# A decoder trunk on one core: the fourth gate and up group moved ahead of the first down groups, every middle block turned by DMA

## The chip, the cores and the metric

The kernel runs on one core of one Trainium2 chip. The metric is device time in microseconds for one execution of the whole program, the median over runs; smaller is better. Engine names are the profile's: PE is TensorE's matmul, PEld its weight load, DVE is VectorE, ACT is ScalarE, POOL is GpSimd, SP is SyncE, whose queue issues almost all DMAs here. "L420" is line 420 of the kernel before.

## The reference

Two pre-norm residual layers over 256 positions of width 2048, in float32. Each layer has a mixer (layer 0: sliding-window attention beside an mLSTM; layer 1: forgetting attention) and a SwiGLU feed-forward block (FFN) with 5632 hidden columns. Only the FFN is touched:

```python
D_MODEL = 2048
SEQ = 256
DEPTH = 2
FFN_HIDDEN = -(-(8 * D_MODEL) // (3 * 256)) * 256      # 5632

def swiglu(xn, w_gate, w_up, w_down):
    return (jax.nn.silu(xn @ w_gate) * (xn @ w_up)) @ w_down

def reference(...):
    h = x
    for layer in range(DEPTH):
        ...
        h = h + mix.astype(h.dtype)
        h = h + swiglu(rms_norm(h, norm_ffn[layer]), w_gate[layer], w_up[layer], w_down[layer])
    return rms_norm(h, norm_final)
```

## The kernel before

**Precision.** Every float32 operand is split into a high and a low half (`hi`, `lo` for weights; `xh`, `xl` for the normed input; `mh`, `ml` for the hidden block), and a product takes three matmuls of 128 rows by 512 columns (`three`, L417 to L420). ACT casts the high half (L167, L293), DVE subtracts for the low half (L168, L294). So each weight chunk of 512 KB (two k tiles by 512 columns) costs an ACT and a DVE instruction before PE can use it.

**Groups.** `pair_group` multiplies 256 rows by two blocks of 512 columns at once. It walks over pairs of k tiles in a given order of positions; a position is either plain (24 matmuls) or mixed (a Strassen-like form with 21 matmuls, more ACT and DVE work, and sums of the left operand, `sx` or `sd`, that must be ready). In the plain positions the results gather in four PSUM banks, `plain`; the mixed ones also fill four banks `prods` of the other half of PSUM. The argument `par` says which half; consecutive groups alternate. At the end the `prods` are evicted into the tile `c` (L549 on ACT, L550 to L553 on DVE). The tile `c` has one buffer.

**The FFN.** The hidden width is eleven blocks of 512 columns. A gate and up group (eight positions, five plain and three mixed, 183 matmuls) makes one block: after it `plain` is added to `c` (L578), SiLU is taken (L580) and gate times up is formed (L582). The block then has to be turned, since the down product contracts over it. `PARTS = (0, 3, 7, 11)` cuts the eleven blocks into three parts. Each part runs its gate and up groups, then two down groups (columns 0 to 1023 and 1024 to 2047 of the output) that contract over the blocks of the part and add into the residual `h` (L675, L299). Part one has three blocks, twelve k tiles, and so down groups of six positions (four plain, two mixed, 138 matmuls); parts two and three have four blocks, and down groups of eight positions.

**Two ways to turn a block.** The usual way is by DMA: ACT copies the 16-bit halves of `c` apart into `flat` (L605, twice), SP issues two DMA transposes (`turn_planes`, L246), and later a closure `join` puts the halves together on ACT (L251, twice), splits them into `mh` and `ml` (L293, L294) and forms the sums `sd` (`sums_of`, L235 to L238). `join` is issued at position `MID` (6) of the next gate and up group, or at `MID_DOWN` (5) of the part's first down group. The last block of part one alone (`g == g1 - 1 and nk < 16`, L585) goes another way: PE transposes it against the identity in eight instructions (L591) into two banks `pf`, and ACT and DVE split from there.

**Order.** The program is written in the order just told; the framework's scheduler sets the order of the instructions on each engine ahead of time, by a simulated time line, so that matmuls of neighbouring groups are interleaved where operands are not ready. On the chip each engine runs its own list in that fixed order. Weight loads and DMA transposes share SP's queue.

Of the kernel before, what the change touches and what calls it, by code (L numbers as in the profile page):

```python
# [17 lines left out]
P = 128  # L18
# [5 lines left out]
NB = 512  # L24
# [23 lines left out]
TURN_AT = (1, 2, 3, 5)  # L48
TURN_DOWN = (2, 3, 4, 6)
MID = 6  # L50
MID_DOWN = 5
RAWS = 4
PARTS = (0, 3, 7, 11)


def mixed_of(order):
    return [p for w, p in order if w]
# [5 lines left out]
def trunk(  # L63
# [96 lines left out]
    def load_chunk(w, k0, c0, n):  # L160
        raw = ahead.pop(0) if ahead else load_raw(w, k0, c0, n)
        return split_chunk(raw, n)
# [129 lines left out]
    def split_plain(dst_h, dst_l, src):  # L292
        nc.scalar.copy(dst_h, src)  # L293
        nc.vector.tensor_tensor(out=dst_l, in0=src, in1=dst_h.bitcast(F32), op=ALU.subtract)  # L294
# [127 lines left out]
    def bank(par, name):  # L422
        return pm.tile([P, NB], F32, tag="pm", name=name) if par else pa.tile([P, NB], F32, tag="acc", name=name)
# [66 lines left out]
            )  # L490
        sums_of(room, sh, sl, None, full)

    def pair_group(room, par, lhs, sums, mats, order, todo=()):
        plain = [[bank(par, "acc") for _ in range(NT)] for _ in range(2)]
        todo = list(todo)
        prods = None
        kinds = [kind for kind, _ in order]
        t0, t1 = slice(0, P), slice(P, 2 * P)
        for pos, (kind, pair) in enumerate(order):
            k0 = 2 * pair  # L500
            if not kind:
                last = pos == len(order) - 1
                walk = [(i, t) for i in range(CK) for t in range(NT)]
                if last:
                    walk.sort(key=lambda it: it[1])
                for m, (w, c0) in enumerate(mats):
                    hi, lo = load_chunk(w, k0, c0, NB)
                    run_due(todo, pos)
                    for i, t in walk:
                        ah, al = lhs(k0 + i)  # L510
                        ts = slice(t * P, (t + 1) * P)
                        three(
                            plain[m][t], ah[:, ts], al[:, ts], hi[:, i, :], lo[:, i, :],
                            pos == 0 and i == 0, last and i == CK - 1,
                        )
                continue
            first, last = 1 not in kinds[:pos], 1 not in kinds[pos + 1 :]
            if first:
                prods = [bank(1 - par, "prod") for _ in range(4)]
            ra, rb = (room.raw(m, w, k0, c0) for m, (w, c0) in enumerate(mats))  # L520
            hg, lg = split_chunk(ra, NB)
            run_due(todo, pos)
            t4 = room.t4()
            nc.vector.tensor_tensor(out=t4[:, 0, :], in0=rb[:, 0, :], in1=ra[:, 0, :], op=ALU.subtract)
            nc.vector.tensor_tensor(out=t4[:, 1, :], in0=rb[:, 1, :], in1=rb[:, 0, :], op=ALU.subtract)
            hu = wp.tile([P, CK, NB], F32R, tag="hi", name="hi")
            lu = wp.tile([P, CK, NB], F32R, tag="lo", name="lo")
            split_plain(hu[:, 1, :], lu[:, 1, :], rb[:, 1, :])
            nc.vector.tensor_tensor(out=rb[:, 0, :], in0=rb[:, 1, :], in1=t4[:, 0, :], op=ALU.subtract)
            nc.vector.tensor_tensor(out=rb[:, 1, :], in0=ra[:, 1, :], in1=rb[:, 0, :], op=ALU.subtract)  # L530
            ht, lt = [], []
            for two in (t4, rb):
                hs, ls = room.two()
                split_plain(hs, ls, two)
                ht += [hs[:, 0, :], hs[:, 1, :]]
                lt += [ls[:, 0, :], ls[:, 1, :]]
            sh, sl = sums(pair)
            xa, la = lhs(k0)
            xb, lb = lhs(k0 + 1)
            three(prods[0], xa[:, t0], la[:, t0], hg[:, 0, :], lg[:, 0, :], first, last)  # L540
            three(plain[0][0], xb[:, t0], lb[:, t0], hg[:, 1, :], lg[:, 1, :], False, False)
            three(plain[1][0], sh[:, 3, :], sl[:, 3, :], hu[:, 1, :], lu[:, 1, :], False, False)
            three(prods[1], sh[:, 0, :], sl[:, 0, :], ht[0], lt[0], first, last)
            three(prods[2], sh[:, 2, :], sl[:, 2, :], ht[1], lt[1], first, last)
            three(prods[3], sh[:, 1, :], sl[:, 1, :], ht[2], lt[2], first, last)
            three(plain[0][1], xb[:, t1], lb[:, t1], ht[3], lt[3], False, False)
        c = room.c()
        u2 = room.tmp([P, NB], "u2")
        nc.scalar.copy(c[:, 0, :], prods[0])  # L549
        nc.vector.tensor_tensor(out=u2, in0=prods[3], in1=c[:, 0, :], op=ALU.add)  # L550
        nc.vector.tensor_tensor(out=c[:, 1, :], in0=prods[2], in1=u2, op=ALU.add)  # L551
        nc.vector.tensor_tensor(out=c[:, 2, :], in0=prods[1], in1=u2, op=ALU.add)
        nc.vector.tensor_tensor(out=c[:, 3, :], in0=prods[1], in1=c[:, 1, :], op=ALU.add)  # L553
        return plain, c

    def ffn(layer, fp, room, pending, sx, sd, key, idx_next=None, key_next=None, finish=None, then=None):
# [3 lines left out]
            j = mixed_of(ORDER).index(pair)  # L560
            return sx[0][:, j, :, :], sx[1][:, j, :, :]

        for g0, g1 in zip(PARTS, PARTS[1:]):
            end = g1 == PARTS[-1]
            nk = 4 * (g1 - g0)
            order = DOWN[nk // 2]
            todo = list(zip(TURN_AT, pending))
            pending = []
            for g in range(g0, g1):
                par = (g1 - 1 - g) % 2  # L570
                plain, c = pair_group(
                    room, par, x_of, sums_x, [(w_gate[layer], g * NB), (w_up[layer], g * NB)], ORDER, todo
                )
                todo = []
                for m in range(2):
                    for t in range(NT):
                        o = c[:, 2 * m + t, :]
# [3 lines left out]
                for t in range(NT):  # L581
                    nc.vector.scalar_tensor_tensor(  # L582
                        out=c[:, t, :], in0=c[:, 2 + t, :], scalar=r[:, t : t + 1], in1=c[:, t, :], op0=ALU.mult, op1=ALU.mult
                    )
                if g == g1 - 1 and nk < 16:  # L585
                    for half in range(2):
                        pt = bank(par, "pf").rearrange("p (i q) -> p i q", i=2)
                        for i in range(2):
                            cs = (2 * half + i) * P
                            for t in range(NT):  # L590
                                nc.tensor.transpose(pt[:, i, t * P : (t + 1) * P], c[:, t, cs : cs + P], ident)  # L591
                        pair = 2 * (g - g0) + half
                        k = 2 * pair
                        split_plain(mh[:, k : k + 2, :], ml[:, k : k + 2, :], pt)
                        if pair in mixed_of(order):
                            j = mixed_of(order).index(pair)
                            sums_of(
                                room, sd[0][:, j, :, :], sd[1][:, j, :, :], lambda full, pt=pt: nc.scalar.copy(full, pt)
                            )
                    continue  # L600
                cu = c.bitcast(U16).rearrange("p a (n b) -> p a n b", b=2)
                flat = c[:, 2:4, :].bitcast(U16).rearrange("p a n -> p (a n)").rearrange("p (b n) -> p b n", b=2)
                turned = [fp.tile([P, 8, P], U16, tag="tmp", name="turned") for _ in range(2)]
# [1 line left out]
                    nc.scalar.copy(flat[:, b, :].rearrange("p (t n) -> p t n", t=NT), cu[:, 0:2, :, b])  # L605
                turn_planes(turned, flat)

                def join(c=c, turned=turned, g=g, g0=g0, order=order):
                    ct = c[:, 0:2, :].rearrange("p a n -> p (a n)")
                    cb = ct.bitcast(U16).rearrange("p (n b) -> p n b", b=2)  # L610
                    join_planes(cb, turned)
                    k = 4 * (g - g0)
                    split_plain(
                        mh[:, k : k + 4, :].rearrange("p k s -> p (k s)"), ml[:, k : k + 4, :].rearrange("p k s -> p (k s)"), ct
                    )
                    for half in range(2):
                        pair = 2 * (g - g0) + half
                        if pair in mixed_of(order):
                            j = mixed_of(order).index(pair)
                            sums_of(  # L620
                                room,
                                sd[0][:, j, :, :],
                                sd[1][:, j, :, :],
                                None,
                                ct[:, half * 512 : (half + 1) * 512].rearrange("p (i t q) -> p i t q", i=2, t=NT),
                            )

                todo = [(MID if g < g1 - 1 else MID_DOWN, join)]

            def sums_d(pair, order=order):  # L630
                j = mixed_of(order).index(pair)
                return sd[0][:, j, :, :], sd[1][:, j, :, :]

            def close(acc, n):
# [12 lines left out]
            for n0 in (0, 2):  # L647
                if end and idx_next is None and n0 == 2:
# [4 lines left out]
                    continue  # L653
                plain, c = pair_group(
                    room,
                    1 - n0 // 2,
                    m_of,
                    sums_d,
                    [(wd, n0 * NB), (wd, (n0 + 1) * NB)],
                    DOWN_END if end and n0 == 2 else order,  # L660
                    todo + list(zip(TURN_DOWN, pending[0::2] + pending[1::2])),
                )
                todo = []
                pending = []
                if end and idx_next is None:
# [641 lines left out]
```

## Time and profile before

| | |
|---|---|
| median of three runs | 2095.85 us (2094.71 to 2096.68) |
| the profiled execution, its own time | 2093.9 us |
| its span in the profile | 2092.2 us |
| PE busy | 2078.2 us, 99% of the span |
| DVE busy | 1809.4 us, 86% |
| ACT busy | 1358.4 us, 65% |
| DMA transposes issued for the tile `c` | 52 |

The busy time of PE is that of overlapping, pipelined instructions, so it hides what matters here: the distance between the starts of neighbouring matmuls. A row of the time line reads: start, duration, engine, line, operation, tiles, how many instructions are merged in the row, and in brackets how long the engine sat idle before it and which instruction released it. A row of the table by windows reads: the window, its length, and for each engine the busy time and the number of instructions, then the granted TensorE clock and the DMA engines' share.

### The profile page before, as it was taken

What the parts mean: (1) busy time and instruction counts of PE and PEld (TensorE: products, weight loads), DVE (VectorE), ACT (ScalarE), POOL (GpSimd) and SP (SyncE); (2) the same over time, 40 slices, a digit from 0 to 9 for tenths busy, and PEclk for the clock granted to TensorE, in tenths of its full rate; (3) what the DMA queues carried; (4) which work ended last, traced back from release to release, by engine and by line L of the source; (5) the groups of instructions that cost most, each with busy time, mean ns of one, the idle gap of its engine ahead of it and who ended that gap; (6) DMA issues with size and microseconds to landing.
All of it is one profiled execution on the core that took longest, in us unless ns stands there. A gap on an engine that the chain in (4) does not pass through costs nothing.

```text
span 2092.2 us, 26777 instructions
## 1 busy us (share of the span) xinstructions
PE 2078.2 (99%) x9518; PEld 1725.2 (82%) x9518; DVE 1809.4 (86%) x2402; ACT 1358.4 (65%) x1717; POOL 42.0 (2%) x70
## 2 busy tenths in 40 slices
PE   9999999999999999999999999999999999999998
PEld 8878888888888888888888888888888888888886
DVE  6689758998999999998899777679989999999995
ACT  7565568665577656666867676587655667556763
POOL 2100000000000000000000000000000000000000
PEclk9999999999999999999999999999999999999999
DMA  9446667766576657676787775677757676657663
GB/s 332 122 133 211 206 194 225 246 195 197 187 232 220 218 193 226 207 222 173 203 258 200 207 212 170 191 233 229 231 168 228 199 222 211 221 191 229 214 204 128
DMA packets 300214, 433.51 MB, mean 207 GB/s; under 512 B 97825, under 2 KB 106033, under 8 KB 300081
## 3 DMA queue, kind: packets, MB, share of 16 engines
q1 hardware_dynamic: 298320, 426.00, 66.0%
q0 software_dynamic: 1616, 5.78, 0.9%
q8 instruction: 74, 1.21, 0.2%
q14 instruction: 60, 0.48, 0.1%
q10 hardware_dynamic: 144, 0.03, 0.0%
HBM read 408.67 MB, written 2.11 MB: 196 GB/s over the span
## 4 chain that ended last, share of the span: by engine, by line
PE 94%; DVE 3%; issue 1%; DMA 1%; ACT 1%; POOLq 0%; POOL 0%; SPq 0%; ACTq 0%; DVEq 0%
PE acc L418 20%; PE acc L419 20%; PE acc L420 20%; PE prod L418 5%; PE prod L420 5%; PE prod L419 5%; PE acc L195 5%; PE acc L197 5%; PE acc L196 5%; PE vacc L195 1%; PE vacc L196 1%; PE vacc L197 1%; DVE lo L168 1%; PE p L324 0%; DMA raw<-in_w_in_even_dram 0%
## 5 line engine op out<-in xcount | busy, mean ns | idle before, releaser
L167 ACT CAST hi<-raw 128x1024 fp32r<-128x1024 f32 (+1 forms) x664 | 675.1, 1031 | 437.8 <-PE acc L420 223.7
L168 DVE TENSOR_TENSOR lo<-raw,hi 128x1024 fp32r<-128x1024 f32 (+1 forms) x664 | 784.2, 1196 | 137.7 <-ACT hi L167 136.2
L419 PE MATMUL acc<-lo,xh 128*128 128x512 f32 x1204 | 468.7, 389 | 0.5 <-DVE lo L168 0.5
L420 PE MATMUL acc<-hi,xl 128*128 128x512 f32 x1204 | 465.7, 389 | 0.0
L418 PE MATMUL acc<-hi,xh 128*128 128x512 f32 x1204 | 463.2, 390 | 0.8 <-DVE c L551 0.8
L418 PEld LDWEIGHTS acc<-hi,xh 128*128 128x128 f32 x1204 | 225.9, 188 | 49.2 <-DVE c L551 1.6
L419 PEld LDWEIGHTS acc<-lo,xh 128*128 128x128 f32 x1204 | 226.0, 188 | 47.9 <-DVE lo L168 0.8
L420 PEld LDWEIGHTS acc<-hi,xl 128*128 128x128 f32 x1204 | 226.0, 188 | 47.2 <-issue 0.3
L419 PE MATMUL acc<-lo,mh 128*128 128x512 f32 x444 | 172.8, 389 | 0.0
L420 PE MATMUL acc<-hi,ml 128*128 128x512 f32 x444 | 171.3, 389 | 0.0
L418 PE MATMUL acc<-hi,mh 128*128 128x512 f32 x444 | 169.6, 389 | 0.0
L293 ACT CAST ht<-t 128x1024 fp32r<-128x1024 f32 x94 | 98.9, 1052 | 52.7 <-PE prod L420 44.6
L293 ACT CAST ht<-raw 128x1024 fp32r<-128x1024 f32 x94 | 98.7, 1050 | 45.0 <-PE acc L420 17.9
L195 PE MATMUL acc<-hi,mh 128*128 128x512 f32 x320 | 125.9, 396 | 0.7 <-ACT mh L293 0.7
L196 PE MATMUL acc<-lo,mh 128*128 128x512 f32 x320 | 124.9, 390 | 0.0
L197 PE MATMUL acc<-hi,ml 128*128 128x512 f32 x320 | 124.5, 392 | 0.0
L294 DVE TENSOR_TENSOR lt<-raw,ht 128x1024 fp32r<-128x1024 f32 x94 | 114.4, 1217 | 10.8 <-ACT ht L293 10.8
L294 DVE TENSOR_TENSOR lt<-t,ht 128x1024 fp32r<-128x1024 f32 x94 | 114.3, 1216 | 5.0 <-ACT ht L293 4.9
L293 ACT CAST hi<-raw 128x512 fp32r<-128x512 f32 x112 | 69.3, 619 | 73.5 <-PE acc L420 53.9
L419 PEld LDWEIGHTS acc<-lo,mh 128*128 128x128 f32 x444 | 83.3, 188 | 17.3
L418 PEld LDWEIGHTS acc<-hi,mh 128*128 128x128 f32 x444 | 83.3, 188 | 17.3
L420 PEld LDWEIGHTS acc<-hi,ml 128*128 128x128 f32 x444 | 83.3, 188 | 17.2
(380 smaller groups left out, 3558.6 us busy)
## 6 DMA issues: line engine op xcount, KB each, us to landing
raw<-in_w_gate_dram SPq DMA_DIRECT2D x176, 512.0 KB, 4.7
raw<-in_w_up_dram SPq DMA_DIRECT2D x176, 512.0 KB, 4.8
raw<-in_w_down_dram SPq DMA_DIRECT2D x176, 512.0 KB, 4.9
raw<-in_w_in_odd_dram SPq DMA_DIRECT2D x88, 512.0 KB, 4.8
raw<-in_w_in_even_dram SPq DMA_DIRECT2D x64, 512.0 KB, 4.8
raw<-in_w_out_even_dram SPq DMA_DIRECT2D x32, 512.0 KB, 4.2
raw<-in_w_out_odd_dram SPq DMA_DIRECT2D x32, 512.0 KB, 4.7
raw<-in_w_in_odd_dram SPq DMA_DIRECT2D x8, 272.0 KB, 3.5
```

Source lines behind the costliest of these rows:

```text
L167: latest[0] = nc.scalar.copy(hi[:, :, 0:n], raw[:, :, 0:n])
L168: nc.vector.tensor_tensor(out=lo[:, :, 0:n], in0=raw[:, :, 0:n], in1=hi[:, :, 0:n].bitcast(F32), op=ALU.subtract)
L195: nc.tensor.matmul(o, ah[:, ts], hi, start=(k == 0), stop=False)
L196: nc.tensor.matmul(o, ah[:, ts], lo, start=False, stop=False)
L197: last_mm[0] = nc.tensor.matmul(o, al[:, ts], hi, start=False, stop=(k == k_all - 1))
L293: nc.scalar.copy(dst_h, src)
L294: nc.vector.tensor_tensor(out=dst_l, in0=src, in1=dst_h.bitcast(F32), op=ALU.subtract)
L418: nc.tensor.matmul(o, ah, hi, start=start, stop=False)
L419: nc.tensor.matmul(o, ah, lo, start=False, stop=False)
L420: nc.tensor.matmul(o, al, hi, start=False, stop=stop)
```

## The change

The order of the groups in a layer becomes gate and up 0, 1, 2, 3; the down groups of part one; gate and up 4, 5, 6; the down groups of part two; gate and up 7 to 10; the down groups of part three. Group 3 belongs to part two still: only its place moves. The branch with the PE transposes is gone; the blocks 2 and 3 are turned by DMA as the others. The block that is finished last before a pair of down groups is joined in the first of them, at position 4 in part one and at position 5 in the others.

Since block 3 is turned while the down groups of part one still read k slots 0 to 11 of `mh` and `ml`, it goes to slots 12 to 15, and blocks 4, 5 and 6 to slots 0 to 11: the k slots of part two are rotated by four, the down weights are read at row `(k + 4) % 16`, and the order of positions in part two (`DOWN_TURNED`) leaves block 6 for last. `par` simply alternates. The number of matmuls in the groups, of weight loads and of sums is the same.

```diff
-MID_DOWN = 5
+MID_DOWN = (4, 5, 5)
 RAWS = 4
 PARTS = (0, 3, 7, 11)
+PASS = ((0, 1, 2, 3), (4, 5, 6), (7, 8, 9, 10))
+DOWN_TURNED = ((0, 0), (0, 1), (1, 2), (0, 3), (1, 6), (0, 7), (1, 4), (0, 5))
...
-    def pair_group(room, par, lhs, sums, mats, order, todo=()):
+    def pair_group(room, par, lhs, sums, mats, order, todo=(), row=lambda k: k):
...
-                    hi, lo = load_chunk(w, k0, c0, NB)
+                    hi, lo = load_chunk(w, row(k0), c0, NB)
...
-        for g0, g1 in zip(PARTS, PARTS[1:]):
+        par, todo = 0, list(zip(TURN_AT, pending))
+        pending = []
+        for part, (g0, g1) in enumerate(zip(PARTS, PARTS[1:])):
             end = g1 == PARTS[-1]
             nk = 4 * (g1 - g0)
-            order = DOWN[nk // 2]
-            todo = list(zip(TURN_AT, pending))
-            pending = []
-            for g in range(g0, g1):
-                par = (g1 - 1 - g) % 2
+            order = (DOWN[6], DOWN_TURNED, DOWN[8])[part]
+            for g in PASS[part]:
                 plain, c = pair_group(
                     room, par, x_of, sums_x, [(w_gate[layer], g * NB), (w_up[layer], g * NB)], ORDER, todo
                 )
-                todo = []
+                par = 1 - par
...
-                if g == g1 - 1 and nk < 16:
-                    for half in range(2):
-                        pt = bank(par, "pf").rearrange("p (i q) -> p i q", i=2)
-                        for i in range(2):
-                            cs = (2 * half + i) * P
-                            for t in range(NT):
-                                nc.tensor.transpose(pt[:, i, t * P : (t + 1) * P], c[:, t, cs : cs + P], ident)
-                        pair = 2 * (g - g0) + half
-                        k = 2 * pair
-                        split_plain(mh[:, k : k + 2, :], ml[:, k : k + 2, :], pt)
-                        if pair in mixed_of(order):
-                            j = mixed_of(order).index(pair)
-                            sums_of(
-                                room, sd[0][:, j, :, :], sd[1][:, j, :, :], lambda full, pt=pt: nc.scalar.copy(full, pt)
-                            )
-                    continue
...
+                first = PARTS[1] if PARTS[1] <= g < PARTS[2] else (PARTS[2] if g >= PARTS[2] else 0)
+                slot = (g - first + 3) % 4 if first == PARTS[1] else g - first
...
-                    k = 4 * (g - g0)
+                    k = 4 * slot
...
+                    if slot:
+                        sums_of(
+                            room,
+                            sd[0][:, slot - 1, :, :],
+                            sd[1][:, slot - 1, :, :],
+                            None,
+                            ct[:, 0:512].rearrange("p (i t q) -> p i t q", i=2, t=NT),
+                        )
 
-                todo = [(MID if g < g1 - 1 else MID_DOWN, join)]
+                todo = [(MID if g < PASS[part][-1] else MID_DOWN[part], join)]
...
-                    1 - n0 // 2,
+                    par,
                     m_of,
                     sums_d,
                     [(wd, n0 * NB), (wd, (n0 + 1) * NB)],
                     DOWN_END if end and n0 == 2 else order,
                     todo + list(zip(TURN_DOWN, pending[0::2] + pending[1::2])),
+                    row=lambda k, nk=nk, by=4 * (part == 1): (k + by) % nk,
                 )
+                par = 1 - par
```

More of the change, by code (lines that the diff above doesn't have):

```diff
@@ L519, in pair_group @@
                 prods = [bank(1 - par, "prod") for _ in range(4)]
-            ra, rb = (room.raw(m, w, k0, c0) for m, (w, c0) in enumerate(mats))
+            ra, rb = (room.raw(m, w, row(k0), c0) for m, (w, c0) in enumerate(mats))
             hg, lg = split_chunk(ra, NB)
@@ L606, in ffn, with join @@
                 turn_planes(turned, flat)
-                def join(c=c, turned=turned, g=g, g0=g0, order=order):
+                first = PARTS[1] if PARTS[1] <= g < PARTS[2] else (PARTS[2] if g >= PARTS[2] else 0)
+                slot = (g - first + 3) % 4 if first == PARTS[1] else g - first
+                def join(c=c, turned=turned, slot=slot):
                     ct = c[:, 0:2, :].rearrange("p a n -> p (a n)")
@@ L615, in join, with sums_d @@
                     )
[L616 to L626, printed above, removed]
-                todo = [(MID if g < g1 - 1 else MID_DOWN, join)]
-            def sums_d(pair, order=order):
-                j = mixed_of(order).index(pair)
+                    if slot:
[7 more added lines that the diff above has]
+                todo = [(MID if g < PASS[part][-1] else MID_DOWN[part], join)]
+            def sums_d(pair):
+                j = pair // 2 - 1
                 return sd[0][:, j, :, :], sd[1][:, j, :, :]
```

## The prediction

> **What bounds the kernel now.** First the busy times and the shares of the chain that ended last.
>
> ```profile
> PE 2078.2 (99%) x9518; PEld 1725.2 (82%) x9518; DVE 1809.4 (86%) x2402; ACT 1358.4 (65%) x1717; POOL 42.0 (2%) x70
> PE 94%; DVE 3%; issue 1%; DMA 1%; ACT 1%; POOLq 0%; POOL 0%; SPq 0%; ACTq 0%; DVEq 0%
> ```
>
> PE sets the end, and the change leaves its 512-column matmuls as they are. So the time can fall only where PE runs something else, or where two starts lie further apart than usual. DVE at 86% is the engine that could take over. The windows over a gate and up group, over the first down group of part one in layer 0 (from its first matmul) and over the first down group of part two say how near it is:
>
> ```profile
> 594.00:636.00 42.00, 42.00 (x187) 34.77 (x186) 40.07 (x52) 29.16 (x32) 0.00 (x0) 1.00 0.71 219
> 459.06:490.30 31.24, 30.69 (x139) 25.11 (x138) 27.47 (x39) 16.28 (x20) 0.00 (x0) 1.00 0.59 181
> 690.40:731.90 41.50, 41.50 (x185) 34.35 (x184) 38.58 (x49) 28.16 (x31) 0.00 (x0) 1.00 0.64 205
> ```
>
> DVE is busy 40.07 of 42.00 us beside a gate and up group, 95%, so what it falls behind it makes good slowly. The clock column is 1.00 in all three. PE is full (41.50 of 41.50) where a block is turned by DMA, and 0.55 us short where PE turns it. The time line of PE there, in layer 0 and then, from the last six transposes on, in layer 1:
>
> ```profile
> 473.35 0.38 PE L591 MATMUL pf<-ident,c 128*128 128x128 f32 x2
> ...
> 473.80 0.39 PE L419 MATMUL prod<-lo,mh 128*128 128x512 f32 x1
> ...
> 478.83 0.82 PE L591 MATMUL pf<-ident,c 128*128 128x128 f32 x6
> 479.40 0.47 PE L420 MATMUL acc<-hi,ml 128*128 128x512 f32 x1
> 480.43 0.50 PE L418 MATMUL prod<-hi,mh 128*128 128x512 f32 x1 [0.55 <-ACT mh L293]
> 480.77 0.40 PE L419 MATMUL prod<-lo,mh 128*128 128x512 f32 x1
> ```
>
> ```profile
> 1538.65 0.82 PE L591 MATMUL pf<-ident,c 128*128 128x128 f32 x6
> 1539.22 0.47 PE L420 MATMUL acc<-hi,ml 128*128 128x512 f32 x1
> 1540.25 0.50 PE L418 MATMUL prod<-hi,mh 128*128 128x512 f32 x1 [0.55 <-ACT mh L293]
> 1540.59 0.40 PE L419 MATMUL prod<-lo,mh 128*128 128x512 f32 x1
> ```
>
> The reader should see the chain transposes, cast on ACT, first matmul that uses the cast; and that both layers lose the same behind the six transposes. One more place where PE waits in the FFN is the start of the next gate and up group, in layer 0 and then, much weaker, in layer 1:
>
> ```profile
> 526.60 0.39 PE L419 MATMUL prod<-lo,xh 128*128 128x512 f32 x1
> ...
> 530.00 0.39 PE L420 MATMUL acc<-hi,xl 128*128 128x512 f32 x1
> 530.22 0.39 PE L418 MATMUL acc<-hi,xh 128*128 128x512 f32 x1
> 531.39 0.50 PE L418 MATMUL acc<-hi,xh 128*128 128x512 f32 x1 [0.78 <-DVE c L551]
> ```
>
> ```profile
> 1590.07 0.82 PE L418 MATMUL acc<-hi,xh 128*128 128x512 f32 x2
> 1590.73 0.40 PE L419 MATMUL acc<-lo,xh 128*128 128x512 f32 x1
> ```
>
> From 526.60 to 530.00 there are 15 steps in 3.40 us: 0.227 us is the usual distance. At 530.22 the distance is 1.17 us, 0.94 too much. PE waits for a bank that DVE's eviction L551 gives free; DVE is late there.
>
> **What goes.** In layer 0: from the first two transposes to the second matmul behind them 473.80 - 473.35 = 0.45 us, of which one matmul is 0.227, so 0.22; the six others 479.40 - 478.83 = 0.57; the wait 480.43 - 479.40 - 0.227 = 0.80; the slow restart 480.77 - 480.43 - 0.227 = 0.11. Together 1.70 us. Layer 1 gives 0.57, 0.80 and 0.11 by its rows, and I take its first pair at the 0.22 of layer 0: again 1.70. **Term one: -3.40 us.** All of it lies on PE, the bounding engine, and no matmul takes its place.
>
> **What comes.** Per layer: two copies into `flat`, two joining copies and one wide cast on ACT in place of three narrow ones, some 4 us more by the 1.99 and 2.56 us of the rows below; ACT is busy 16.28 of 31.24 us in that window, so ACT's idle time covers them, and without that cover they would be at most 2 x 4 = 8 us. DVE does one wide subtraction for two narrow ones, no more work. SP gets two DMA transposes. These rows show the same step in part two, with the first matmul of the down group ahead; the last two rows are for part one as it is:
>
> ```profile
> 690.42 0.39 PE L418 MATMUL acc<-hi,mh 128*128 128x512 f32 x1
> 700.12 0.74 DVE L582 SCALAR_TENSOR_TENSOR c<-c,r 128x512 f32<-128x512 f32 x1
> 702.75 1.99 ACT L605 COPY c<-c 128x1024 uint16<-128x1024 uint16 x2
> 703.81 2.62 SPq L246 DMA_TRANSPOSE turned<-c  x2
> 707.50 2.56 ACT L251 COPY c<-turned 128x1024 uint16<-128x1024 uint16 x2
> 715.63 0.28 DVE L238 TENSOR_TENSOR s<-c,s 128x128 f32<-128x128 f32 x1
> 723.80 0.58 ACT L549 COPY c<-prod 128x512 f32<-128x512 f32 x1
> ```
>
> ```profile
> 471.85 0.74 DVE L582 SCALAR_TENSOR_TENSOR c<-c,r 128x512 f32<-128x512 f32 x1
> 482.36 0.59 ACT L549 COPY c<-prod 128x512 f32<-128x512 f32 x1
> ```
>
> The tile `c` has one buffer. From the end of L582 (700.86) to its last reader in the join (715.91) it is held 15.05 us; in part two L549, which overwrites it, comes 7.9 us later and nobody waits. In part one the block would be finished about where it is now, 472.59, so `c` would be free at 487.64, **5.3 us later than L549 starts now** (482.36). What is queued behind L549 are DVE's evictions, and behind these the banks of the second down group. That group needs its first bank 138 x 0.227 = 31.3 us after 459.06, at 490.4; the bank of L549 is free at 487.64 + 0.58 = 488.2. So 2.2 us remain and **term two is 0**. Its bounds: nothing below, and above the slowest join that the trace has:
>
> ```profile
> 863.88 1.99 ACT L605 COPY c<-c 128x1024 uint16<-128x1024 uint16 x2
> ...
> 877.44 2.57 ACT L251 COPY c<-turned 128x1024 uint16<-128x1024 uint16 x2
> ```
>
> There 13.56 us lie between flat and join instead of 4.75, 8.8 more; less the 2.2 in hand that is 6.6 us per layer. I take 0, because the case at 702.75 has the same place (a first down group) and the slow one is in a gate and up group, where the join is put at position 6.
>
> SP's queue is held while it waits for the flat copies, and weight loads stand behind it:
>
> ```profile
> SPq L246 <- ACT c L605: 51.5, 17, 5.5
> ```
>
> That happened 17 times, 3.0 us each, and PE was full in the window at 690.40, which holds one of them; two new ones cost nothing as long as split weights lie ready, and up to 5.5 us each, 11 us together, if none do. I take 0, as in that window.
>
> **What moves.** Group 3 brings its 183 matmuls, 16 weight loads and all its ACT, DVE and DMA-transpose work ahead of the 24 loads of the two down groups; counts and sizes are unchanged, and behind group 2 it offers 41.5 us to hide that block's turn, as after groups 0 and 1. The rotation changes addresses only. The second stall, at 530.22, I ascribe to DVE: it stood idle while ACT waited for PE to free the split buffers, and PE was on its transposes:
>
> ```profile
> 479.93 1.23 DVE L168 TENSOR_TENSOR lo<-raw,hi 128x1024 fp32r<-128x1024 f32 x1 [3.15 <-ACT hi L167]
> ```
>
> 3.15 us lost, in an engine with 5% to spare, come back as lateness 50 us on. Without it the 0.94 us go, and in layer 1 1590.73 - 1590.07 - 2 x 0.227 = 0.20. **Term three: -1.14 us**; bounds -1.14 and +1.14, the second if the two short down groups leave DVE as late again in both layers as it is late now.
>
> A rule of the Trainium skill speaks against the change: VectorE: DVE Perf Modes, Rules for kernel authors, has a 128x128 block transposed on TensorE if it may land in PSUM, and by the DMA crossbar only otherwise; The three transpose paths there puts the DMA at 1309 ns for one 16-bit block. By that figure the 16 blocks of both planes would take an estimated 20.9 us one after another and the kernel would lose about 25 us; the trace has 3.7 us from the issue at 703.81 to the join at 707.50, so it does not agree and I follow the trace.
>
> **Sum.** -3.40 + 0 - 1.14 = -4.54 us. The profiled execution took 2093.9 us (span 2092.2, 1.7 around it), so it would take 2089.4; the median of the runs is 1.95 higher, and on its scale 2095.85 - 4.54 = **2091.3 us**.
>
> **The rivals.**
> *DVE stays late.* The two short groups have two mixed positions in six and the same evictions as long ones, so DVE may enter group 4 as late as it now enters group 3. For: the 95%. Against: part two's pair of down groups ends with no stall. Then only term one counts: 2095.85 - 3.40 = 2092.5.
> *`c` comes free too late.* The place is L549 in the first down group of part one. Once the join ends more than 2.2 us later than in part two, PE stands at the start of the second down group. For: six positions instead of eight, a margin of 2.2 against 7.9 us. Against: the scheduler can draw matmuls of other positions forward. At the slowest join: 2 x 6.6 - 3.40 = +9.8, 2105.7; at half of that wait +3.2, 2099.1. The skill's rule above would act through this very place.
> *It does not do what it says.* PE's transposes go, but their 1.70 us per layer come back as waits elsewhere in the FFN, since DVE at 95% cannot feed PE faster. For: the chain runs over DVE in 3% of the span. Against: full PE in the long groups. Time 2095.9.
>
> **How the numbers follow.** About 0.2%, 4.2 us, is what a measurement of this kernel can tell from no change. Forecast 0.50 (0.44 beyond 4.2 us, 0.06 within); DVE stays late 0.22 (0.03 and 0.19); does not do what it says 0.08, within; late `c` 0.20, all slower. Faster 0.47, same 0.33, slower 0.20. The forecast's own range is 2089.2 to 2092.5: below, the lowest run of before is 1.1 under the median, and I allow 1 us for waits of the mixer in layer 1 that a shifted schedule may drop. The range goes up to the half-price case of late `c`, rounded to 2099.5, and leaves out about half of that rival.
>
> **What would show it.** Right: L591 and the tile `pf` gone, 16 PE instructions fewer, no PE wait on ACT's `mh` in the FFN, 56 transposes from `c` instead of 52; L549 of the first down group near 28.6 us after that group's first matmul with no gap at the second group; no wait on L551 at the start of group 4. Wrong: a gap of over 1 us at the start of the second down group or of group 4, or a PE wait on the split of weights behind the new DMA transposes.

## The result and the profile after

The kernel after took 2092.58 us, median of 22 runs (2089.5 to 2096.03), against 2095.86 us for the kernel before (22 runs, 2093.6 to 2097.91): a ratio of 0.9984 with a 95% interval of [0.9978, 0.9991]. In a later series the same two kernels gave 2091.92 (11 runs) against 2096.52 (15 runs), 0.9979 [0.997, 0.9988]. Both intervals lie below 1, so it is faster, if little: by 0.16 to 0.21%, 3.3 and 4.6 us; the forecast was 4.5. (The prediction took 4.2 us for the least that can be told from no change; the first series, 22 runs of each kernel, tells 3.3.)

Lines of the kernel after lie two further down up to the evictions: L549 of before is L551 there, L418 to L420 are L420 to L422, L167 is L169, L293 is L295, L251 is L253; L582 is L583 and L605 is L590. The profiled execution took 2096.03 us, with a span of 2094.3 and a mean granted clock of 0.996. **It is 2.1 us longer than the one of before** (2092.2, clock 0.999), though the median fell. First the two lines of the page of after, busy times and shares of the chain:

```profile
PE 2080.2 (99%) x9502; PEld 1727.9 (83%) x9502; DVE 1810.2 (86%) x2400; ACT 1365.8 (65%) x1721; POOL 41.1 (2%) x70
PE 94%; DMA 2%; DVE 2%; ACT 1%; issue 1%; SPq 0%; POOLq 0%; POOL 0%; ACTq 0%
```

PE has 16 instructions fewer, ACT 7.4 us more work, DVE is as before; in the chain DVE has 2% instead of 3% and DMA 2% instead of 1%. The tile `turned<-c` has 56 transposes instead of 52. The waits of PE in after (who waited, on what; total, times, longest):

```profile
PE acc L197 <- ACT mh L295: 3.1, 2, 2.2
PE pw L135 <- POOL ones L131: 1.1, 1, 1.1
PE acc L198 <- DVE lo L170: 0.8, 2, 0.4
PE acc L421 <- DVE lo L170: 0.5, 1, 0.5
```

L420 to L422 are the three matmuls of `three`, which the FFN shares with other products. They have no wait on `mh` here, and none on an eviction of `c`; their one wait on a split stands at 136.5 us, in layer 0's mixer (at 136.0 us in before). The waits of L197 and L198 are ahead of the FFN or in the mixers. To price the FFN without the rest, take two events that exist in both kernels and lie on either side of the moved groups: the ACT eviction behind gate and up group 1, and the one behind group 7. The ACT time line of before, then of after, layer 0 and layer 1:

```profile
408.32 0.61 ACT L549 COPY c<-prod 128x512 f32<-128x512 f32 x1
...
805.82 0.57 ACT L549 COPY c<-prod 128x512 f32<-128x512 f32 x1
...
1468.43 0.58 ACT L549 COPY c<-prod 128x512 f32<-128x512 f32 x1
...
1864.81 0.57 ACT L549 COPY c<-prod 128x512 f32<-128x512 f32 x1
```

```profile
411.97 0.58 ACT L551 COPY c<-prod 128x512 f32<-128x512 f32 x1
...
806.32 0.58 ACT L551 COPY c<-prod 128x512 f32<-128x512 f32 x1
...
1472.84 0.58 ACT L551 COPY c<-prod 128x512 f32<-128x512 f32 x1
...
1867.19 0.58 ACT L551 COPY c<-prod 128x512 f32<-128x512 f32 x1
```

Before: 397.50 and 396.38 us. After: 394.35 and 394.35. **The changed stretches got 3.15 and 2.03 us shorter, 5.18 together**; ahead of the first event and from the eviction behind group 10 on, the order of the instructions on every engine is the same in both kernels. In between, in groups 8 and 9, some instructions change places; up to the eviction behind group 10 the differences are 3.13 and 2.02 us, so nothing hangs on these. The execution lost the 5.18 and 2.1 more elsewhere. Four places. At 146.8 us the granted clock falls to one half behind matmuls with four rows (`pb<-mt,sel`). The same 8 us, from the first of these matmuls on, by windows, in after and then in before (length; busy time and count of PE, PEld, DVE, ACT, POOL; clock; DMA share; GB/s):

```profile
145.60:153.60 8.00, 8.00 (x23) 5.93 (x23) 6.73 (x21) 5.48 (x13) 0.00 (x0) 0.57 0.00 0
```

```profile
145.10:153.10 8.00, 8.00 (x36) 6.38 (x36) 6.90 (x21) 5.49 (x13) 0.00 (x0) 1.00 0.00 0
```

Thirteen matmuls fewer in the same time, at 0.227 us each: 3.0 us, with PE "busy" for all 8.00 us in both. The next two places follow one another in the mixer of layer 1. The time line of PE and ACT there, in after and then in before:

```profile
1310.58 0.39 PE L199 MATMUL acc<-hi,ml 128*128 128x512 f32 x1
1311.58 1.04 ACT L169 CAST hi<-raw 128x1024 fp32r<-128x1024 f32 x1 [2.49 <-DMA raw<-in_w_out_odd_dram]
1312.53 1.07 ACT L295 CAST mh<-po 128x512 fp32r<-128x512 f32 x2
1313.16 0.50 PE L197 MATMUL acc<-hi,mh 128*128 128x512 f32 x1 [2.19 <-ACT mh L295]
...
1314.23 0.63 PE L197 MATMUL acc<-hi,mh 128*128 128x512 f32 x1
1314.66 0.63 PE L198 MATMUL acc<-lo,mh 128*128 128x512 f32 x1
```

```profile
1309.86 1.05 ACT L167 CAST hi<-raw 128x1024 fp32r<-128x1024 f32 x1 [2.20 <-DMA raw<-in_w_out_odd_dram]
1310.81 1.06 ACT L293 CAST mh<-po 128x512 fp32r<-128x512 f32 x2
1311.44 0.50 PE L195 MATMUL acc<-hi,mh 128*128 128x512 f32 x1 [0.69 <-ACT mh L293]
```

In both kernels PE waits for the cast `mh<-po`, and on ACT that cast stands behind a weight cast whose load is not there: the engine's list is in order, so a cast that could run waits for a DMA that it does not need. The wait is 2.36 us too long in after (1313.16 - 1310.58 - 0.227) and 0.86 in before by the same reckoning: 1.5 us. Behind it the clock is at one half for 3.4 us (steps of 0.43 instead of 0.227, eight of them: 1.6 us). The fourth place is of the same kind: in after, L197 at 1344.35 us waits 0.88 us for another cast of `mh`, which on ACT stands behind a weight cast that waited 3.53 us for its load; in before the same matmul (1339.94) does not wait. It costs 1.1 us. So 3.0 + 1.5 + 1.6 + 1.1 = 7.2 of the 7.3 us.

### The profile page after: what moved, and what is told of

Its sections match the earlier page's. It is cut to its first block, busy times and chain, and to the rows that moved or that the text cites. A ratio compares the mean times of both kernels' runs of the same rounds, so it can differ in the third digit from the quotient of the medians.

```text
span 2094.3 us, 26757 instructions
## 1 busy us (share of the span) xinstructions
PE 2080.2 (99%) x9502; PEld 1727.9 (83%) x9502; DVE 1810.2 (86%) x2400; ACT 1365.8 (65%) x1721; POOL 41.1 (2%) x70
## 4 chain that ended last, share of the span: by engine, by line
PE 94%; DMA 2%; DVE 2%; ACT 1%; issue 1%; SPq 0%; POOLq 0%; POOL 0%; ACTq 0%
PE acc L421 20%; PE acc L420 20%; PE acc L422 20%; PE prod L420 5%; PE prod L421 5%; PE prod L422 5%; PE acc L197 4%; PE acc L199 4%; PE acc L198 4%; PE vacc L199 1%; PE vacc L197 1%; PE vacc L198 1%; DMA raw<-in_w_out_odd_dram 1%; DVE lo L170 1%; PE p L326 0%
## 5 line engine op out<-in xcount | busy, mean ns | idle before, releaser
L169 ACT CAST hi<-raw 128x1024 fp32r<-128x1024 f32 (+1 forms) x664 | 674.4, 1031 | 430.0 <-PE acc L422 247.9
L422 PE MATMUL acc<-hi,xl 128*128 128x512 f32 x1204 | 464.7, 389 | 0.0
L420 PE MATMUL acc<-hi,xh 128*128 128x512 f32 x1204 | 462.1, 389 | 0.0
L422 PEld LDWEIGHTS acc<-hi,xl 128*128 128x128 f32 x1204 | 226.1, 188 | 47.2 <-issue 0.3
L420 PEld LDWEIGHTS acc<-hi,xh 128*128 128x128 f32 x1204 | 226.1, 188 | 46.9
L422 PE MATMUL acc<-hi,ml 128*128 128x512 f32 x444 | 171.4, 389 | 0.0
L420 PE MATMUL acc<-hi,mh 128*128 128x512 f32 x444 | 169.3, 389 | 0.0
L295 ACT CAST ht<-raw 128x1024 fp32r<-128x1024 f32 x94 | 98.8, 1051 | 58.9 <-DVE raw L532 22.4
L197 PE MATMUL acc<-hi,mh 128*128 128x512 f32 x320 | 126.6, 398 | 3.1 <-ACT mh L295 3.1
L198 PE MATMUL acc<-lo,mh 128*128 128x512 f32 x320 | 125.7, 393 | 0.0
L295 ACT CAST ht<-t 128x1024 fp32r<-128x1024 f32 x94 | 98.8, 1052 | 39.6 <-PE prod L422 29.3
L295 ACT CAST hi<-raw 128x512 fp32r<-128x512 f32 x112 | 69.3, 619 | 63.9 <-PE acc L422 48.6
L420 PEld LDWEIGHTS acc<-hi,mh 128*128 128x128 f32 x444 | 83.3, 188 | 17.3
L422 PEld LDWEIGHTS acc<-hi,ml 128*128 128x128 f32 x444 | 83.3, 188 | 17.3
```

The costliest lines, as they stand in the source:

```text
L169: latest[0] = nc.scalar.copy(hi[:, :, 0:n], raw[:, :, 0:n])
L197: nc.tensor.matmul(o, ah[:, ts], hi, start=(k == 0), stop=False)
L198: nc.tensor.matmul(o, ah[:, ts], lo, start=False, stop=False)
L420: nc.tensor.matmul(o, ah, hi, start=start, stop=False)
L422: nc.tensor.matmul(o, al, hi, start=False, stop=stop)
```

## The experiments

"Stretches" are the two distances above, layer 0 and layer 1, in the profile of a run.

**Do the transposes cause both stalls?** The kernel before, with block 2 not turned at all: its casts read `c` as it stands, so that the eight PE transposes per layer are left out, and with them the two banks `pf`. What the kernel then computes is not the reference.

```diff
-                        pt = bank(par, "pf").rearrange("p (i q) -> p i q", i=2)
-                        for i in range(2):
-                            cs = (2 * half + i) * P
-                            for t in range(NT):
-                                nc.tensor.transpose(pt[:, i, t * P : (t + 1) * P], c[:, t, cs : cs + P], ident)
+                        pt = c[:, half, :].rearrange("p (i q) -> p i q", i=2)
```

> The order of before; block 2 of part one is split as it lies, not turned (its turn is left out), so PE's eight transposes and the banks pf are gone and nothing else. Measured in the profile: the stretch from the eviction L549 of group 1 to that of group 7, 397.50 us in layer 0 and 396.38 in layer 1 before, 394.35 in both after the change. Theory (DVE is late at the start of group 3 because it idled while PE was on its transposes and waited for the cast): no wait on L551 at the start of group 3, both stretches 394.3 to 394.6. Rival (the two short down groups make DVE late by themselves): the 0.94 us and 0.20 us stay, 395.8 in layer 0 and 394.8 in layer 1.

Measured: stretches 394.36 and 394.38, those of after; 2090.77 us in one run, beside 2097.64 for the kernel before (nine runs). All waits of PE in it:

```profile
PE pw L133 <- POOL ones L129: 1.1, 1, 1.1
PE acc L195 <- ACT mh L293: 1.1, 1, 1.1
PE acc L195 <- ACT hi L167: 1.1, 1, 1.1
PE acc L419 <- DVE lo L168: 0.6, 1, 0.6
PE acc L196 <- DVE lo L168: 0.5, 1, 0.5
```

The wait on `mh` behind the transposes is gone, and so is the one on L551 50 us later, with the order of before. So the second stall comes with the turn by PE and not with the order of the groups; how it comes is told below, at term three. And turning block 2 by DMA, as the change does, costs nothing more than not turning it.

**One half of the change alone.** First the turn by DMA in the order of before, joined at position 3 of the down group:

```diff
-                if g == g1 - 1 and nk < 16:
...
-                    continue
...
-                todo = [(MID if g < g1 - 1 else MID_DOWN, join)]
+                todo = [(MID if g < g1 - 1 else (3 if nk < 16 else MID_DOWN), join)]
```

> The order of before; block 2 of part one is turned by DMA and joined at position 3 of the first down group, where position 4 needs it. Theory (the moved group is what hides the turn): block 2 is split some 27 to 29 us after the first down matmul and needed at 93 x 0.227 = 21.1 us, so PE stands 6 to 8 us per layer in part one: stretches 400 to 403 us, time 2103 to 2109. Rival (the turn by DMA is the gain, the order a matter of taste): stretches 394.4 us, time 2091 to 2093.

Measured: 2108.03 us, ratio 1.0054 [1.004, 1.0068]; stretches 402.47 and 402.11. The PE time line:

```profile
481.83 0.39 PE L420 MATMUL acc<-hi,ml 128*128 128x512 f32 x1
487.57 0.80 PE L418 MATMUL prod<-hi,mh 128*128 128x512 f32 x1 [5.35 <-ACT mh L293]
```

PE runs out of matmuls that do not need block 2, waits 5.51 us in each layer, and then goes at half the clock (from 486.0 and 1551.0 on) for 6.8 us. Block 2 needs a gate and up group behind it.

Then the order of after, with block 2 turned by PE:

```diff
+                if g == 2:
+                    for half in range(2):
+                        pt = bank(1 - par, "pf").rearrange("p (i q) -> p i q", i=2)
...
+                        split_plain(mh[:, k : k + 2, :], ml[:, k : k + 2, :], pt)
...
+                    continue
```

> The order after the change, with group 3 ahead of the down groups of part one; block 2 is turned by PE as before, block 3 by DMA. Theory (three terms: transposes 0.79, wait and restart 0.91, late DVE 1.48 and 0.32): the wait and the late DVE go, the transposes stay: stretches 395.1 us in both layers, 0.8 more than with the change, and a time 1.6 us above the changed kernel's, 2092 to 2095. Rival (late DVE follows the transposes wherever they are): a wait of about 1 us at one of the next two groups, stretch of layer 0 396 us or more.

Measured: 2104.71 us, ratio 1.0037 [1.0023, 1.0051]; stretches 401.41 and 399.50. A miss: the expectation had it faster than before. No wait stands at the transposes, but there is a large one where none was expected, at the start of part one's second down group (DVE, PE and ACT in order of time):

```profile
524.20 0.76 DVE L583 SCALAR_TENSOR_TENSOR c<-c,r 128x512 f32<-128x512 f32 x1
538.01 0.39 PE L422 MATMUL acc<-hi,ml 128*128 128x512 f32 x1
541.52 0.58 ACT L551 COPY c<-prod 128x512 f32<-128x512 f32 x1
542.15 0.79 PE L420 MATMUL acc<-hi,mh 128*128 128x512 f32 x1 [3.75 <-ACT c L551]
```

PE needs the bank at 538.01 + 0.227 = 538.24 and gets it at 542.15, 3.9 us late, and 6.8 us at half the clock follow (2.3 us and 1.0 in layer 1, where the clock stays whole). This is the place of the rival "`c` comes free too late". The delay starts earlier: gate times up of block 3 ends at 524.96, 13.3 us ahead of that need, against 17.2 us in after (518.03 and 535.21, rows below). Up to there the two kernels differ by PE's transposes and the casts behind them; that these leave DVE and ACT late through the whole of group 3, so that the turn of block 3 by DMA inherits it, I read from the rows (DVE's first eviction of group 3, L552, starts at 508.33, 29.9 us ahead of the need, and at 503.16 in after, 32.05 ahead), and no run tried it alone.

**Is `c` really that close?** The kernel after, with the two joining copies of block 3 run twice, so that ACT gets about 2.7 us more work inside the join. Nothing else is changed in the program; in the lists that the scheduler makes of it, two weight casts more also stand ahead of L551 on ACT:

```diff
-                    join_planes(cb, turned)
+                    for _ in range(2 if slot == 3 and first == PARTS[1] else 1):
+                        join_planes(cb, turned)
```

> The changed kernel; the joining copies of block 3 in the first down group of part one run twice (the same bytes again), which holds the tile c some 2.4 us longer. In the changed kernel the eviction L551 of that group starts 30.1 us after its first matmul and the second group needs the bank at 31.3, so 0.6 us are in hand. Theory of the prediction's third rival (late c makes PE stand): L551 at 32 to 33 us, a gap of 1 to 2.5 us at the start of the second down group, stretches 395.5 to 397 us. Its rival (matmuls of other positions are drawn forward): stretches 394.4 us as with the change.

Measured: stretches 399.90 and 398.14, 2101.99 us in one run. The time line of DVE, PE and ACT:

```profile
518.09 0.76 DVE L583 SCALAR_TENSOR_TENSOR c<-c,r 128x512 f32<-128x512 f32 x1
535.80 0.39 PE L422 MATMUL acc<-hi,ml 128*128 128x512 f32 x1
538.32 0.57 ACT L551 COPY c<-prod 128x512 f32<-128x512 f32 x1
538.95 0.80 PE L420 MATMUL acc<-hi,mh 128*128 128x512 f32 x1 [2.76 <-ACT c L551]
```

L551 starts 19.47 us after gate times up (518.85), 3.46 later than in after (534.04 - 518.03 = 16.01), and PE stands for 538.95 - 535.80 - 0.227 = 2.92 us: of 3.46 us of delay 0.5 were covered. The gap was larger than the 1 to 2.5 us expected, and so were the stretches (in layer 0 with 0.9 us at 424 us, ahead of the doubled join, and about 1.8 us of half clock behind the wait). The rival's mechanism is real; after runs just in front of it.

**Was the time given back outside the FFN chance?** Both kernels were profiled twice more, unchanged.

> The changed kernel once more, unchanged. Outside the stretch from group 1 to group 7 of each layer every engine's list of instructions is the same in both kernels, so theory (what the profile of after lost outside the two stretches is chance: late landings of w_out_odd and half-clock windows that come in some executions of either kernel): stretches 394.35 us again, and fewer or other half-clock windows than at 146.8 and 1314.1 us; time 2090 to 2092. Rival (the shift in time makes the wait before the cast of mh at 1310 us longer and the half clock regular): the wait is again over 2 us there, the half-clock windows lie where they lay, time 2092.5 to 2094.

> The kernel before once more, for its profile. Theory (chance outside the stretches): stretches 397.5 and 396.4 us again within 0.1; a wait at 1310 us that is not 0.86 us again, and perhaps a half-clock window. Rival (the profile of before is typical, and only the changed kernel has these windows): 0.8 to 0.9 us at 1310 and a clock of 1.00 from 6 us to the end.

> The kernel before, a third profile. The wait of PE on the cast of mh in layer 1's mixer was 0.86 and 0.72 us in its first two profiles, 2.36 and 1.50 in the two of the changed kernel. Theory (chance of a landing load): somewhere between 0.7 and 2.4 us, on either side of 1.2. Rival (the earlier end of layer 0's FFN makes the wait longer): 0.7 to 0.9 us again.

> The changed kernel, a third profile. Theory (chance of a landing load): the wait on the cast of mh in layer 1's mixer lies between 0.7 and 2.4 us, on either side of 1.2. Rival (the earlier end of layer 0's FFN makes the wait longer): 1.2 us or more again. Both: stretches 394.2 to 394.4 us.

The account of the three pairs, in us ("mixer wait" is the excess at the first matmul on `mh<-po` in layer 1; "half clock" what its windows cost more in after than in before):

| pair | span before | span after | difference | stretches | mixer wait | half clock | rest |
|---|---|---|---|---|---|---|---|
| first profiles | 2092.2 | 2094.3 | +2.1 | -5.18 | 0.86 to 2.36: +1.50 | +4.6 | +1.2 |
| second | 2094.2 | 2090.0 | -4.2 | -5.55 | 0.72 to 1.50: +0.79 | one window each | +0.6 |
| third | 2095.0 | 2089.7 | -5.3 | -5.05 | 1.17 to 2.03: +0.86 | one window each | -1.1 |

Both stretches together are steady: 788.7, 788.5 and 788.7 us in after, 793.9, 794.05 and 793.7 in before. By layer those of before are less so, 397.50 and 396.38, then 397.12 and 396.93, then 397.02 and 396.73: e7's "within 0.1" was a miss. What spoilt the first pair is the half clock, which comes and goes within one and the same kernel, and the wait at 1344 us. The first profile of before is the only one of the twelve in which the clock stays whole up to the last microseconds.

The mixer's wait on that cast was longer in after in all three pairs, 1.50 to 2.36 us against 0.72 to 1.17. That speaks for the rival, that the change makes it longer (e9's 2.03 fits it; e5's 1.50 is under the 2 us and e8's 1.17 over the 0.9 us that it named); the change would then lose 0.8 to 1.5 us outside the FFN. But by the same reckoning e2, with the order of before, has 1.79 us there, and e3 and e4, with the order of after, have 1.39 each. Whether the change itself makes it longer is open.

**The mixer's wait taken away.** The kernel after, with the weight chunks of the first six k tiles for the second output block issued behind the cast of `mh` for the third heads, instead of ahead of it:

```diff
+        last_cast[0] = nc.scalar.copy(dst_h, src)
...
+            last_pv[0] = last_cast[0]
...
+        pv2 = last_pv[0]
...
-        begin(1, 0, 6)
+        with tc.issue_after(pv2.ins):
+            begin(1, 0, 6)
```

> The changed kernel; in layer 1's mixer the casts of the weights for the second output block are put behind the cast of mh for the third heads on ACT, so that mh no longer stands behind a cast that waits for a load of w_out_odd. Theory (that one wait costs 0.86 us in the profile of before, 2.36 in that of after, and its idle time brings a half-clock window that costs 1.6 more): no PE wait on mh at 1310 us, no half-clock window behind it, 1 to 3 us faster than the changed kernel, 2088 to 2091. Rival (the load is late anyway and PE waits for the weights a little later): the wait moves by some matmuls, time as the changed kernel's within 0.5 us.

> The kernel of the run e6_cast_first (the changed kernel with the weight casts of layer 1's mixer put behind the cast of mh) once more. Theory: 0.9963 of the kernel before again, within 0.995 to 0.9975, no wait on that cast. Rival (a lucky set of runs): as the changed kernel, 0.998 to 0.9985.

Measured in two series: 2089.53 us, ratio to the kernel before 0.9963 [0.995, 0.9975], and 2089.35, 0.9965 [0.9951, 0.9978]; the kernel after in the first of them 2091.92 (11 runs), in the second 2091.45 (one run). Stretches 394.35, four times. The ACT time line of the first (lines lie two further down again, L295 is L297):

```profile
1306.09 0.59 ACT L297 CAST mh<-po 128x512 fp32r<-128x512 f32 x1 [0.32 <-PE po L382]
1307.39 0.59 ACT L297 CAST mh<-po 128x512 fp32r<-128x512 f32 x1 [0.72 <-PE po L382]
...
1308.60 2.01 ACT L171 CAST hi<-raw 128x1024 fp32r<-128x1024 f32 x2
```

Now the casts wait for PE's `po` and for nothing else, the weight cast comes behind, and no wait of PE on `mh` is left in either profile. The 2.4 and 2.1 us are about the wait of 1.5 to 2.4 us. This version is the fastest measured; the intervals of the two ratios overlap with that of after, while the medians differ the same way both times.

The join of block 3 at another position of the down group was not tried.

## Why the prediction was right, and where it was off

**Term one, -3.40 us: right.** The transposes, the wait on the cast and the slow restart are gone in both layers, and nothing takes their place: the stretches of after have no wait of PE on `mh`. e1 has the same stretches without any turn.

**Term three, -1.14 us: right that the stall goes, wrong in how it came about, too small in size.** The stall on the eviction goes with the turn by PE (e1), not with the order. The prediction held that 3.15 us of idle time at 479.93 come back as lateness of DVE. But an engine that is only late is busy, and DVE stands idle just ahead of the late eviction. The time line of DVE in before:

```profile
526.23 0.68 DVE L550 TENSOR_TENSOR u<-prod,c 128x512 f32<-128x512 f32 x1
528.84 0.69 DVE L524 TENSOR_TENSOR t<-raw 128x512 f32<-128x512 f32 x1 [1.93 <-issue]
529.45 0.69 DVE L525 TENSOR_TENSOR t<-raw 128x512 f32<-128x512 f32 x1
530.05 0.68 DVE L294 TENSOR_TENSOR lo<-raw,hi 128x512 fp32r<-128x512 f32 x1
530.65 0.68 DVE L551 TENSOR_TENSOR c<-prod,u 128x512 f32<-128x512 f32 x1
```

L524 needs a weight chunk whose load SP issued at 523.47 us; by the trace's DMA events it landed at 528.76, the wait of L524 for it on DVE ends at 528.80, and L524 starts at 528.84. The eviction L551 has its operand `u` from 526.91 on, but it stands behind L524, L525 and L294 in DVE's list: the same pattern as on ACT in the mixer. The stall follows that load. In the three profiles of before the load took 5.29, 5.14 and 5.06 us from issue to landing in layer 0 and 4.45, 5.03 and 4.82 in layer 1, and PE lost 0.94, 0.79 and 0.71, and 0.20, 0.68 and 0.47: each time the flight less 4.25 to 4.35 us. In e1 the list has L551 (525.97) ahead of L524 (527.77). In after L526 and L527 still stand ahead of L553, but the chunk is there and DVE does not wait (568.50). DVE's lateness can be the first cause all the same: from 474 us up to L550 it waits 6.0 us in before (0.61, 3.15 and 2.28) and 3.8 in e1 (0.34, 3.14 and 0.31), and the load is issued when DVE has freed the buffer, at 523.44. No run separates the two.

The sum of the steps was 4.54 us, the three pairs have 5.05 to 5.55. The difference is the slow restart behind this stall, 0.11 in layer 0, which the sum left out; 0.28 at 420.5 us, in group 2, in the first profile of before alone; the longer stall of layer 1 in the other two; and about 0.1 us per layer that I did not place.

**Term two, 0: right in the sum, wrong in its margin.** The step predicted L549 28.6 us after the group's first matmul and 2.2 us in hand. The time lines of PE, DVE and ACT in after:

```profile
503.93 0.39 PE L420 MATMUL acc<-hi,mh 128*128 128x512 f32 x1
517.29 0.74 DVE L583 SCALAR_TENSOR_TENSOR c<-c,r 128x512 f32<-128x512 f32 x1
533.20 0.28 DVE L240 TENSOR_TENSOR s<-c,s 128x128 f32<-128x128 f32 x1
533.51 0.62 ACT L295 CAST sd<-s 128x512 fp32r<-128x512 f32 x1 [0.32 <-DVE s L240]
534.04 0.58 ACT L551 COPY c<-prod 128x512 f32<-128x512 f32 x1
535.21 0.39 PE L420 MATMUL acc<-hi,mh 128*128 128x512 f32 x1
```

L551 starts 30.11 us after 503.93; its bank is free at 534.62 and needed at 535.21: **0.6 us in hand** (0.58 to 0.70 in both layers of the five profiles of after, e6 and e10). The 1.53 us are three small things. Gate times up ends 14.10 us after the first matmul and not 13.53 as in before (+0.57). `c` is held 15.45 us, to 533.48, and not the 15.05 of part two (+0.40). And L551 does not start when `c` is free: the cast of `sd` stands ahead of it on ACT (+0.56), which I had left out. The windows show what it did to PE, group 3 and then the down group (columns as above):

```profile
461.97:503.40 41.43, 41.43 (x184) 34.32 (x183) 38.83 (x50) 28.48 (x31) 0.00 (x0) 1.00 0.65 206
503.93:535.21 31.28, 31.28 (x139) 25.91 (x138) 28.82 (x38) 22.04 (x25) 0.00 (x0) 1.00 0.67 207
```

PE is full in both, so the term is 0. But the right working would have said 0.6 us, and given "late `c`" more than its chance of 0.20; e4 shows that 3.5 us more ahead of L551 cost 2.9 and 2.8, and e3 that 4.5 us (0.5 in the join, 3.9 ahead of it) cost 3.9. The rival's condition was right, its point wrong: it decides from 0.6 us on.

**SP's queue and ACT at 0: right.** ACT has 7.4 us more work (predicted 8), under PE. No PE wait for a weight split stands behind the new transposes; the one wait of `three` on a split in after, 0.5 us, lies in layer 0's mixer and is in before too.

**The rivals.** "DVE stays late" gave 2092.5, and the first median is 2092.58. By the time alone this rival would be the winner; by the trace it is not, because the stall that it keeps is gone. What brought the first median to its figure lies outside the FFN. And that the medians came out so near the forecast is in part luck: the FFN gained 0.5 to 1 us more than the sum, and the mixer gave 0.8 to 1.5 us back in the three pairs. "Does not do what it says" falls by the same lines.

**What the steps did not hold.** The sum priced the FFN and took the rest of the program as fixed. Its order is fixed up to groups 8 and 9, but not its time: one wait of 0.7 to 2.4 us in the mixer and half-clock windows of 3.4 or 6.8 us move by as much as the change is worth. The 1 us by which the range allowed for the mixer was on the wrong side: its wait was longer in after, not shorter.

## What to carry to other kernels

When a tile with one buffer changes its path, count to the instruction that overwrites it, with everything that stands ahead of that on its in-order engine; part two's length of the hold alone made a margin of 0.6 us look like 2.2. Measure a small change between two events that frame it in both kernels: here the whole span said +2.1 where the stretch said -5.2, and the stretch was steady to 0.3 us. And look on the in-order engines for an instruction that is ready behind one that waits for a load: turning two around brought half as much as the whole change. The stall that term three put down to a busy DVE was of this kind too; the idle time just ahead of the late instruction tells the one from the other.

## What the runs showed of the hardware

**The half clock sits on a fixed raster.** Within each profile the starts of the half-clock stretches lie whole multiples of 3.413 us apart: in after 146.78, 1314.14 and 2088.96 (342.0 and 227.0 steps), in e2 148.09, 486.01, 1550.97 and 2100.52 (99.0, 312.0 and 161.0). Ahead of the program's end they last one step or two, 3.41 or 6.83 us. Cut each long wait of PE at this raster, and the part that falls into one step tells whether the clock drops behind it:

| wait of PE (profile, start) | us in all | most in one step | clock behind it |
|---|---|---|---|
| e9, 1307.8 | 1.87 | 1.87 | half |
| after, 1311.0 | 2.19 | 2.19 | half |
| e3, 538.4 | 3.75 | 2.36 | half |
| e4, 536.2 | 2.76 | 2.67 | half |
| e2, 482.2 | 5.35 | 3.41 | half |
| e4, 1598.7 | 2.68 | 1.76 | full |
| e2, 1318.0 | 1.63 | 0.82 | full |
| e3, 1604.4 | 2.15 | 1.34 | full |
| e5, 1309.4 | 1.34 | 1.34 | full |

So a wait of 2.68 us left the clock alone and one of 1.87 halved it: what counts in these nine is about 1.8 us of idle time within one step. (e2's other long wait, at 1548.8 us, is like its first; six waits of 0.87 to 1.23 us left the clock full.) Where the raster lies against the program differs from run to run. The Trainium skill, TensorE: Matmul & The Clock Gate, Part 1: The HAM clock gate, has a free-running window of 3413 ns, and the traces agree with that length. In the section Why this matters for your kernels of the same page the Trainium skill asks for no idle gaps above about 3 us; here 1.87 us were enough, so by these runs that bound is too wide.

**And without any wait:** in ten of the twelve profiles (not in the first of before, nor in e9) the clock is at one half for one step or two from 146.3 to 148.5 us on. PE is marked busy through it, 8.00 of 8.00 us in the window of after above; the matmuls ahead of it have four rows. That these count as little work for the clock was not tried by itself.
